# Score products of two attention branches: the low-part product over all 128 rows of the array instead of 64

## The chip, the cores and the metric

The kernel runs on one core of one Trainium2 chip. The metric is the time of one execution on the device, in microseconds. The engines of the core are called PE (TensorE, with PEld for its weight loads), DVE (VectorE), ACT (ScalarE), POOL (GpSimd) and SP (SyncE, which here only starts transfers).

## The reference

One step of a two-layer network on 128 context tokens and 512 latent tokens of width 1024. Every layer has a mixing sub-layer and a feed-forward sub-layer, each between two norms and modulated by a conditioning vector. The mixing sub-layer has three branches: A, grouped-query attention in a window (8 query heads, 2 key heads, a learned sink); B, attention over an 8 x 16 neighbourhood of a grid of 64 columns (8 heads, a learned bias); and C, a Fourier transform. All heads have 64 channels. The change is in the scores of branches A and B:

```python
s_band = jnp.einsum('bnqkgd,bnskd->bnkgqs', qb, kb, preferred_element_type=jnp.float32) * scale   # A
s_ctx = jnp.einsum('bnqkgd,bpkd->bnkgqp', qb, ck, preferred_element_type=jnp.float32) * scale
s_loc = jnp.einsum('bnqhd,bmnshd->bhnqms', q_blk, k_reg, preferred_element_type=jnp.float32) * scale  # B
s_ctx = jnp.einsum('bnqhd,bphd->bhnqp', q_blk, ck, preferred_element_type=jnp.float32) * scale
```

Each is followed by a softmax over the local and the context keys together, and by the product with the values.

## The kernel before

All dense products are computed with operands split in two parts: x = hi + lo, where hi has the reduced precision that one pass of the array takes and lo is the rest. A dense product is three passes: hi x hi (L487), hi x lo (L488) and lo x hi (L489), accumulated in one PSUM tile `ps_mm`. Weights arrive in pieces of 128 x 1024 on SP's queue; ACT makes their hi part (L144) and DVE their lo part (L145). Tokens are in two groups, of 384 and 256 columns, so most dense products stream 384 or 256 columns against 128 x 128 weights.

The scores are computed for a pair of heads at a time. `stack_q` (L591) builds `qst`, one 128-row operand for each head h of the pair: the 64 rows of the head's own half hold the hi part of q, the other 64 rows the lo part. A score is then two products into one tile `ps_s`. L547 takes all 128 rows of `qst` against all 128 rows of `khi`: this gives q_hi x k and q_lo x k. L548 takes only the 64 rows of q_hi against the 64 rows of `klo` and adds q_hi x k_lo. So L547 contracts over 128 rows of the array, and L548 over rows 0 to 63 (first head) or 64 to 127 (second head).

A unit of attention is one block of 128 queries for both heads of a pair: L547, L548, L547, L548, on 512, 384 or 128 key columns. There are 80 units: for each of the two layers, four pairs of branch A and four of branch B, with five units each. A unit goes through four steps, each emitted one tick after the other (`tick`, L516): the scores with a reduction on DVE (L549, maximum; POOL negates it in L551), the exponentials (ACT L557, DVE L562 and L564), the transposes of the probabilities (PE L574 into `ps_t`, copied by ACT L578 and DVE L576), and the product with the values (PE L587, which fills 64 columns of the array for each head). The ticks are interleaved with dense products: `step` (L228) counts the dense time that has been emitted, and lets a tick run when 2.5 us have gathered. All engines run their instructions in the order of this emission, which is written by hand.

For a pair of branch B, `queue_b` (L932) prepares the keys and the bias. ACT writes the hi part of the head's own half of `khi` (L940), DVE the lo part in `klo` (L941) and a copy of k in the other half of `khi` (L942). POOL clears a part of the bias tile (L945), starts eight transfers that fill the rest (L949), and adds the column mask (L956). `khi` and `klo` share one pool of two buffers (tag "k7"), so the next pair's `klo` takes the place of the last one's. In branch B `klo` is declared for two heads, and its first slot is used: rows 0 to 63 for the first head and rows 64 to 127 for the second. In branch A, `klo` has the lo part of a key head in both halves of the rows already (L734, L735).

Of the kernel before, what the change touches and what calls it, by code (L numbers as in the profile page):

```python
# [15 lines left out]
L = 2  # L16
# [29 lines left out]
class Null:  # L46
    """Stands for everything while the order of the weights is recorded."""
# [29 lines left out]
class Weights:  # L77
    """Streams pieces of [128, 1024] in the order of their use. A piece is one DMA and, but for raw ones,
    is split into two float32r parts (hi + lo) on chip."""
# [14 lines left out]
    @staticmethod  # L94
    def alt_slot(key):
        """Pieces that are split into a place of their own: of the token-major products the last one of the first half
        and the first one of the second, and what comes first after those products."""
        l, kind, n = key[:3]
        if kind in ("wo", "fo"):
            k0 = 0 if kind == "wo" else DFF // 128 - 8  # L100
            return {(0, k0 + 6): 0, (1, k0): 1}.get(key[2:])
        return 0 if n == 0 and (kind == "fg" or kind == "uc" and l) else None

    @staticmethod
    def is_side(key):
        """Pieces of w_ada that are used beside the feed-forward products have slots of their own."""
        return key[1] == "ada" and (key[0] > 0 or key[2] == 5)
# [68 lines left out]
    def early(self, key):  # L176
        """Moves a piece up in the order of the loads."""
        if self.recording:
            self.get(key)
# [17 lines left out]
class Kernel:  # L197
# [16 lines left out]
    # ---------------------------------------------------------------- order of emission  # L214
# [3 lines left out]
    def run_tasks(self, tags=()):  # L218
        """Those that are due; of some tags all; with tags None all."""
        while True:  # L220
            due = [t for t in self.tasks if tags is None or t[0] <= self.vt or t[2] in tags]
            if not due:
                return
            t = min(due, key=lambda z: z[0])
            self.tasks.remove(t)
            t[1]()

    def step(self, dur):  # L228
        """Called after dense products that take the tensor engine dur microseconds: emits what runs beside them."""
        self.vt += dur  # L230
        self.run_tasks()
        self.ada_acc += dur
        while self.ada is not None and self.ada_acc >= self.ada_dt:
            if next(self.ada, "end") == "end":
                self.ada = None
            self.ada_acc = self.ada_acc - self.ada_dt if self.ada_dt else -1.0
        if self.att_busy():
            self.acc += dur
            if self.acc >= TICK:
                self.acc = 0.0  # L240
                self.tick()

    # ---------------------------------------------------------------- pools
# [10 lines left out]
    # ---------------------------------------------------------------- weights  # L254
    def source(self, key):
        """DRAM pattern [128, a, b] of a piece and its b."""
# [22 lines left out]
    # ---------------------------------------------------------------- setup  # L279
# [34 lines left out]
    # ---------------------------------------------------------------- modulation  # L314
    def ada_round(self, l, r, acc=None):
        """1024 columns of silu(c) @ w_ada + b_ada for both token kinds: rounds 0 and 1 have half each of the first
        two blocks of D columns, the others a block each. Row 32j + s (s: 0 context, 1 latent) of a [128, 256] tile
        holds columns 256 j .. of kind s. With acc [128, 2, 1024] VectorE adds up the row blocks of w_ada, scaled, and
        TensorE only sums over the partitions."""
# [56 lines left out]
    def ada_columns(self, l, r, mod):  # L376
        """Columns of round r as [128, 8, 2]: channel 128 k + p of kind s, as is or (1 + it) * g."""
# [31 lines left out]
    # ---------------------------------------------------------------- norms  # L409
    def rstd(self, a, b=None):  # L410
        """(a + b) ** -0.5; b is EPS unless given."""
# [8 lines left out]
    def open_o(self):  # L420
        """A branch's result, split."""
# [3 lines left out]
    def norm_tiles(self):  # L425
        """Working space for the norms, in the same place."""
        return self.fix.tile([128, 5, D], F32, name="nt", tag="os", bufs=1)

    def pre_sq(self, t, x, z):
        """1 / rms(x[t])"""  # L430
# [4 lines left out]
    def pre_e(self, t, x, z, r):  # L435
        """z = x[t] / rms(x[t])"""
        self.nc.vector.tensor_scalar(z, x[:, t, :], r, None, op0=OP.mult)

    def pre_t1(self, l, sub, t, z, hfs, vec=False):
        """z transposed, by halves of the channels, and modulated."""  # L440
# [19 lines left out]
    def pre_t2(self, t, z, hfs, lo_on=None):  # L460
        """hT[:, t]: its two parts."""
# [8 lines left out]
    def square(self, t, h, src):  # L470
        """Mean square of half h of token tile t."""
# [7 lines left out]
    # ---------------------------------------------------------------- dense  # L479
    def mm_group(self, ps, lhs, rhs, g, K, ks=None):  # L480
        """ps = sum_k lhs_k.T @ rhs_k over the tokens of group g, in three float32r passes."""
# [14 lines left out]
    def proj(self, key, g, evac, parts=1):  # L496
        """128 columns of hT.T @ w for the tokens of group g; evac(psum, g) takes the result."""
# [17 lines left out]
    # ---------------------------------------------------------------- attention pipeline  # L515
# [16 lines left out]
    def drain(self, *key):  # L532
        """Until every unit whose key begins like this is through."""
# [3 lines left out]
    def att_s(self, u):  # L537
# [5 lines left out]
        for h in range(2):  # L543
            ps = self.psum("s")[:, :n]
            r0 = 64 * h
            out = ps if not u["grid"] else ps.rearrange("p (r c) -> p r c", c=32)
            nc.tensor.matmul(out, u["q"][:, h, u["qc"]], u["khi"](h), start=True, stop=False)  # L547
            nc.tensor.matmul(out, u["q"][r0:r0 + 64, h, u["qc"]], u["klo"](h), start=False, stop=True)  # L548
# [42 lines left out]
    def stack_q(self, stage):  # L591
        """Per head of a pair: rows of its own half hold hi, the other half lo."""
# [16 lines left out]
    def rope(self, dst, src, c0, n, scale):  # L609
        """dst = rotated src (PSUM), latent positions c0 .. c0 + n."""  # L610
# [10 lines left out]
    def rope_evac(self, dst, scale, c_lat):  # L621
        """Evacuates 128 rows of transposed q or k: context tokens as they are, latent ones rotated."""
# [8 lines left out]
    # ---------------------------------------------------------------- mixing sub-layer  # L631
# [7 lines left out]
    def mix_open(self, l):  # L639
        """First products on the tokens of group 0, beside the norms of the others."""  # L640
# [7 lines left out]
    def first(self):  # L648
        """The first norm and the first products of the first layer beside the modulation they need, in the order of
        START: A next piece of w_ada, F columns of a round, G / X loads, E moves a piece of uc up, P norm of a token  # L650
        tile, h / H first or second half of its channels modulated, l / L and split, S split of a piece of uc, m / M and
        n / N its products with either half for the tokens of group 0 and 1."""
# [169 lines left out]
    # ---- branch A  # L822
# [15 lines left out]
    def queue_a(self, p):  # L838
# [4 lines left out]
        # key columns (own context, cached, latent, cached), first mask tile and value tiles of each query block  # L843
# [3 lines left out]
        for b, ((k0, k1), m0, vt) in enumerate(spans):  # L847
# [5 lines left out]
                klo=lambda h, k0=k0, k1=k1: klo[64 * h:64 * h + 64, kv, k0:k1],  # L853
# [5 lines left out]
    # ---- branch B; latent columns of q are in blocks of 16 grid columns  # L859
# [72 lines left out]
    def queue_b(self, p):  # L932
# [5 lines left out]
        for h in range(2):  # L938
            a, b = slice(64 * h, 64 * h + 64), slice(64 - 64 * h, 128 - 64 * h)
            nc.scalar.activation(khi[a, h, :], ks[a, :896], AF.Copy)  # L940
            nc.vector.tensor_tensor(klo[a, 0, :], ks[a, :896], khi[a, h, :].bitcast(F32), op=OP.subtract)  # L941
# [18 lines left out]
        for n in range(4):  # L960
# [5 lines left out]
                klo=lambda h, s=s: lat(klo[64 * h:64 * h + 64], 0, s),  # L966
# [6 lines left out]
            khi=lambda h: khi[:, h, 0:128], klo=lambda h: klo[64 * h:64 * h + 64, 0, 0:128],  # L973
# [3 lines left out]
    # ---- branch C  # L977
    def load_dft(self, l):
        """The split position DFT, in the place of m until the branches are merged."""
# [20 lines left out]
    def four1(self, g):  # L1000
        """Channel DFT of group g, the cosine rows 0 .. 64 and the sine rows 1 .. 63 of it (the others are these or
        their negatives), then sums and differences of tokens 256 apart."""
# [31 lines left out]
    def mirror(dst, src):  # L1034
        """Pieces of all rows of a channel DFT, cosines and sines in the order 0 .. 64, 127 .. 65, from 65 + 63 of them."""
# [3 lines left out]
    def four2(self, g):  # L1039
        """Position DFT of group g: even frequencies from the sums, odd ones from the differences."""  # L1040
# [23 lines left out]
    # ---- gates and branch projections  # L1064
    def gates(self, br, ns):
        """tanh(half the gate) for output tiles ns, one group of tokens at a time."""
# [7 lines left out]
    def merge(self, br, n0, hook=None, gates=None):  # L1074
        """Output tiles n0, n0 + 1: m += 2 sigmoid(gate) * (o @ w_branch); the 2 goes when m is split."""
# [37 lines left out]
    # ---------------------------------------------------------------- token-major products  # L1113
# [27 lines left out]
    def xstat(self, keys, lhs, done):  # L1141
        """[128 tokens, 512] = sum of lhs_k[t].T @ w_k over the pieces of each half; done(t, half, psum)."""
# [15 lines left out]
    def xstat_tiles(self, keys, lhs, done):  # L1158
        """The same, with the second half token tile by token tile, so that the tiles end one after the other."""
# [44 lines left out]
    def tail(self, l, sub, t, z):  # L1204
        """x[t] += rms_norm(y) * g_post * gate, from z = y * g_post * gate, and, for sub-layer (l, sub), the next
        modulated norm."""
# [39 lines left out]
    # ---------------------------------------------------------------- feed-forward  # L1246
    def ffn(self, l):
        nc = self.nc
        n0 = 0
        for p, nt in enumerate(FFN_PARTS):  # L1250
# [3 lines left out]
            def split_of(j, aT=aT):  # L1254
                """hi and lo of row block j of the hidden layer."""
# [73 lines left out]
    # ---------------------------------------------------------------- all  # L1329
# [127 lines left out]
```

## Time and profile before

| | |
|---|---|
| median of 3 runs | 2252.7 us (2252.53 to 2252.97) |
| profiled execution, first to last instruction | 2250.8 us |
| the median less the profiled execution | 1.9 us |
| PE busy, PEld busy | 2213.2 us, 2008.8 us |
| DVE, ACT, POOL busy | 1137.3 us, 790.5 us, 337.9 us |
| attention units, first and last start | 124.6 us and 1628.0 us |

The time of the profiled execution is given as its span; what lies around the span in a timed run is the 1.9 us of the third row. A row of the timeline gives the start and the duration in microseconds, then the engine, the line of the kernel, the operation, the tile written and the tiles read, and the shape: for a matmul `64*128 64x384` means 64 rows and 128 columns of the array, and 64 rows by 384 columns of moving data. The matmuls of PE overlap each other, since they are pipelined, and their ends are modelled. What one of them costs the stream is therefore read from start to start.

### The profile page before, as it was taken

To read this page: it belongs to the slowest core of one execution; us is meant where nothing else is said; L and a number is where in the kernel's file an instruction comes from. 1 tells how busy PE (TensorE), PEld (TensorE's weight loads), DVE (VectorE), ACT (ScalarE), POOL (GpSimd) and SP (SyncE) were. 2 spreads that over 40 slices of the span, in tenths; PEclk is the share of its full clock that TensorE was granted. 3 is DMA by queue.
4 is the path that set the end of the run, shared out by engine and by line. 5 is a ranking of instruction groups with operands and counts; after the bars stand their busy time and mean duration, and the time that the engine had idled before them with its cause. 6 is when DMAs were issued, how large, how long until landed. Compare 5 with 4: busy or idle time off the path is not lost. (4 is left out here: it accounts for less than half of the span.)

```text
span 2250.8 us, 35153 instructions
## 1 busy us (share of the span) xinstructions
PE 2213.2 (98%) x14260; PEld 2008.8 (89%) x14260; DVE 1137.3 (51%) x2025; ACT 790.5 (35%) x1640; POOL 337.9 (15%) x619
## 2 busy tenths in 40 slices
PE   6999999999999999999989999999999999999998
PEld 4988899998879899899879888999998898998996
DVE  3554564553356566666466555645443662332343
ACT  3634443432243222112256344434333522221221
POOL 3100123231121000000041002222211400000002
PEclk9999999999999999999999999999999999999999
DMA  7311123233644444443332112233324142222221
GB/s 264 115 48 47 52 66 89 70 89 122 208 134 157 133 140 141 150 141 108 108 107 84 43 57 58 65 80 73 79 66 159 40 158 75 76 76 75 76 80 71
DMA packets 250049, 223.78 MB, mean 99 GB/s; under 512 B 10016, under 2 KB 209728, under 8 KB 249632
## 3 DMA queue, kind: packets, MB, share of 16 engines
q1 hardware_dynamic: 243408, 209.60, 30.1%
q0 software_dynamic: 6048, 11.68, 2.5%
q8 instruction: 113, 1.85, 0.3%
q14 instruction: 48, 0.39, 0.1%
q10 hardware_dynamic: 432, 0.25, 0.0%
HBM read 214.91 MB, written 6.59 MB: 98 GB/s over the span
## 5 line engine op out<-in xcount | busy, mean ns | idle before, releaser
L487 PE MATMUL ps_mm<-hT_hi,whi 128*128 128x256 f32 (+1 forms) x2832 | 890.9, 315 | 1.5 <-DVE sg L1098 1.0
L489 PE MATMUL ps_mm<-hT_hi,wlo 128*128 128x256 f32 (+1 forms) x2832 | 877.2, 310 | 0.8 <-DVE wlo L145 0.7
L488 PE MATMUL ps_mm<-hT_lo,whi 128*128 128x256 f32 (+1 forms) x2832 | 876.6, 310 | 0.0
L487 PEld LDWEIGHTS ps_mm<-hT_hi,whi 128*128 128x128 f32 x2832 | 533.0, 188 | 20.1 <-issue 15.1
L489 PEld LDWEIGHTS ps_mm<-hT_hi,wlo 128*128 128x128 f32 x2832 | 532.8, 188 | 1.6 <-DVE wlo L145 1.6
L488 PEld LDWEIGHTS ps_mm<-hT_lo,whi 128*128 128x128 f32 x2832 | 533.1, 188 | 0.2
L145 DVE TENSOR_TENSOR wlo<-wraw,whi 128x1024 fp32r<-128x1024 f32 x253 | 312.5, 1236 | 413.1 <-ACT whi L144 411.6
L144 ACT ACTIVATE whi<-wraw 128x1024 fp32r<-128x1024 f32 x253 | 266.9, 1056 | 285.6 <-PE ps_mm L1138 170.4
L1136 PE MATMUL ps_mm<-whi,aT 128*128 128x512 f32 x400 | 158.5, 396 | 0.0
L1138 PE MATMUL ps_mm<-whi,aT 128*128 128x512 f32 x400 | 157.9, 395 | 0.0
L1137 PE MATMUL ps_mm<-wlo,aT 128*128 128x512 f32 x400 | 157.8, 395 | 0.0
L1272 ACT ACTIVATE aT<-sg 128x384 fp32r<-128x384 f32 x88 | 41.5, 471 | 259.3 <-DVE sg L1270 259.3
L1071 ACT ACTIVATE sg<-ps_mm 128x384 f32<-128x384 f32 x96 | 41.7, 436 | 236.9 <-PE ps_mm L489 236.7
L350 DVE SCALAR_TENSOR_TENSOR ada_acc<-ada_raw,ada_st,ada_acc 128x1024 f32<-128x1024 f32 x98 | 123.6, 1280 | 0.0
L487 PE MATMUL ps_mm<-o,whi 128*128 128x256 f32 (+1 forms) x384 | 122.5, 319 | 0.0
L488 PE MATMUL ps_mm<-o,whi 128*128 128x256 f32 (+1 forms) x384 | 118.9, 310 | 0.0
L489 PE MATMUL ps_mm<-o,wlo 128*128 128x256 f32 (+1 forms) x384 | 118.8, 309 | 0.0
L1266 ACT ACTIVATE sg<-ps_mm 128x384 f32<-128x384 f32 (+1 forms) x88 | 38.5, 438 | 194.8 <-PE ps_mm L489 194.8
L477 POOL TENSOR_SCALAR ss<-ss 128x1 f32<-128x1 f32 x20 | 6.7, 336 | 603.6 <-ACT junk L475 602.8
L1267 DVE SCALAR_TENSOR_TENSOR sg<-sg,ps_mm 128x384 f32<-128x384 f32 (+1 forms) x88 | 42.9, 487 | 104.4 <-ACT sg L1266 104.4
L557 ACT ACTIVATE P<-P,sm 128x384 f32<-128x384 f32 (+2 forms) x160 | 92.8, 584 | 5.4 <-POOL sm L551 5.4
L1136 PEld LDWEIGHTS ps_mm<-whi,aT 128*128 128x128 f32 x400 | 75.2, 188 | 18.5 <-ACT aT L1272 0.8
(207 smaller groups left out, 2883.4 us busy)
## 6 DMA issues: line engine op xcount, KB each, us to landing
wraw<-in_w_in SPq DMA_DIRECT2D x92, 512.0 KB, 3.9
wraw<-in_w_ffn_in SPq DMA_DIRECT2D x88, 512.0 KB, 3.8
ada_raw<-in_w_ada SPq DMA_DIRECT2D x56, 512.0 KB, 4.4
wraw<-in_w_ffn_out SPq DMA_DIRECT2D x44, 512.0 KB, 3.5
wraw<-in_w_ada SPq DMA_DIRECT2D x40, 512.0 KB, 4.7
wraw<-in_w_branch SPq DMA_DIRECT2D x24, 512.0 KB, 3.5
wraw<-in_w_out SPq DMA_DIRECT2D x16, 512.0 KB, 4.0
bias<-in_b_rpbT POOLq DMA_DIRECT2D x64, 96.0 KB, 4.8
```

The source lines that it names most:

```text
L144: nc.scalar.activation(hi[:, :u.n], u.raw[:, :u.n], AF.Copy)
L145: nc.vector.tensor_tensor(lo[:, :u.n], u.raw[:, :u.n], hi[:, :u.n].bitcast(F32), op=OP.subtract)
L350: nc.vector.scalar_tensor_tensor(acc[:, s, :], u.raw, c, acc[:, s, :], op0=OP.mult, op1=OP.add)
L487: nc.tensor.matmul(ps, wh, xh[:, c0:c1], start=(k == 0), stop=False)
L488: nc.tensor.matmul(ps, wh, xl[:, c0:c1], start=False, stop=False)
L489: nc.tensor.matmul(ps, wl, xh[:, c0:c1], start=False, stop=(k == K - 1))
L557: nc.scalar.activation(P[:, h, :n], P[:, h, :n], AF.Exp, bias=sm[:, 2 + h:3 + h], accum_out=sm[:, 4 + h:5 + h])
L1071: lambda ps, g: self.nc.scalar.activation(sg[:, GROUPS[g][0]:GROUPS[g][1]], ps, AF.Tanh, scale=0.5))
L1136: nc.tensor.matmul(ps, xh[:, tc], u.hi[:, i, :], start=st and i == 0, stop=False)
L1137: nc.tensor.matmul(ps, xh[:, tc], u.lo[:, i, :], start=False, stop=False)
L1138: nc.tensor.matmul(ps, xl[:, tc], u.hi[:, i, :], start=False, stop=sp and i == 1)
L1267: nc.vector.scalar_tensor_tensor(t, t, 1.0, ps, op0=OP.add, op1=OP.mult)
```

## The change

In both branches L548 (L547 in the new numbering) takes all 128 rows of `qst` and all 128 rows of `klo`. In branch A this adds the product q_lo x k_lo, since `klo` has the lo part in both halves. In branch B `klo` uses both of its slots, one for each head: the head's own half gets the lo part as before, and the other half is set to zero by a new POOL instruction, 64 x 896, for each head. Comments and docstrings are taken out as well, which moves no instruction; from line 545 on, line numbers are smaller by one up to line 940, and the same as before from line 942 on.

```diff
     def att_s(self, u):
         ...
         for h in range(2):
             ps = self.psum("s")[:, :n]
-            r0 = 64 * h
             out = ps if not u["grid"] else ps.rearrange("p (r c) -> p r c", c=32)
             nc.tensor.matmul(out, u["q"][:, h, u["qc"]], u["khi"](h), start=True, stop=False)
-            nc.tensor.matmul(out, u["q"][r0:r0 + 64, h, u["qc"]], u["klo"](h), start=False, stop=True)
+            nc.tensor.matmul(out, u["q"][:, h, u["qc"]], u["klo"](h), start=False, stop=True)
...
     def queue_a(self, p):
         ...
-                klo=lambda h, k0=k0, k1=k1: klo[64 * h:64 * h + 64, kv, k0:k1],
+                klo=lambda h, k0=k0, k1=k1: klo[:, kv, k0:k1],
...
     def queue_b(self, p):
         ...
         for h in range(2):
             a, b = slice(64 * h, 64 * h + 64), slice(64 - 64 * h, 128 - 64 * h)
             nc.scalar.activation(khi[a, h, :], ks[a, :896], AF.Copy)
-            nc.vector.tensor_tensor(klo[a, 0, :], ks[a, :896], khi[a, h, :].bitcast(F32), op=OP.subtract)
+            nc.vector.tensor_tensor(klo[a, h, :], ks[a, :896], khi[a, h, :].bitcast(F32), op=OP.subtract)
+            nc.gpsimd.memset(klo[b, h, :].bitcast(F32), 0.0)
             nc.vector.tensor_copy(khi[b, h, :], ks[a, :896])
...
-                klo=lambda h, s=s: lat(klo[64 * h:64 * h + 64], 0, s),
+                klo=lambda h, s=s: lat(klo, h, s),
...
-            khi=lambda h: khi[:, h, 0:128], klo=lambda h: klo[64 * h:64 * h + 64, 0, 0:128],
+            khi=lambda h: khi[:, h, 0:128], klo=lambda h: klo[:, h, 0:128],
```

The order of POOL's instructions at the preparation of the first pair of branch B, before (the last transfers of the values, then the bias; in brackets the engines and queues that an instruction waits for):

```order
L913 DMA vbt<-in_c_cvb 128x128 [waits PE_49]
L913 DMA vbt<-in_c_cvb 128x128 x2
L945 MEMSET bias 128x6x128
L949 DMA bias<-in_b_rpbT 16x6x256
L949 DMA bias<-in_b_rpbT 16x6x256 [waits DMASW2_49]
```

The same place in the changed kernel:

```order
L912 DMA vbt<-in_c_cvb 128x128 [waits PE_49]
L912 DMA vbt<-in_c_cvb 128x128 x2
L941 MEMSET klo 64x896 [waits PE_49,Pool_49]
L941 MEMSET klo 64x896
L945 MEMSET bias 128x6x128 [waits Pool_49]
L949 DMA bias<-in_b_rpbT 16x6x256
L949 DMA bias<-in_b_rpbT 16x6x256 [waits DMASW2_49]
```

Two instructions per pair stand ahead of the bias, 16 in all, and the first of them waits for PE.

The order of PE's instructions at the first unit of that pair, before (the end of one dense product, the unit, the start of the next):

```order
L489 MATMUL ps_mm<-hT_hi,wlo 128x384
L547 MATMUL ps_s<-khi,qst 128x384 [waits DVE_49,Activation_49]
L548 MATMUL ps_s<-klo,qst 128x384
L547 MATMUL ps_s<-khi,qst 128x384 [waits DVE_49,Activation_49]
L548 MATMUL ps_s<-klo,qst 128x384
L487 MATMUL ps_mm<-hT_hi,whi 128x256 [waits DVE_49,PE_49]
```

In the changed kernel:

```order
L489 MATMUL ps_mm<-hT_hi,wlo 128x384
L546 MATMUL ps_s<-khi,qst 128x384 [waits DVE_49,Activation_49]
L547 MATMUL ps_s<-klo,qst 128x384 [waits Pool_49]
L546 MATMUL ps_s<-khi,qst 128x384 [waits DVE_49,Activation_49]
L547 MATMUL ps_s<-klo,qst 128x384 [waits Pool_49]
L487 MATMUL ps_mm<-hT_hi,whi 128x256 [waits DVE_49,PE_49]
```

The order is the same; in the first unit of each pair of branch B, the two low-part products also wait for POOL. (The order gives the output's shape, so that 64 or 128 rows of contraction read alike.)

## Prediction

> **What bounds the kernel now.** I read the page first: busy shares, slices, and the chain that ended last.
>
> ```profile
> span 2250.8 us, 35153 instructions
> PE 2213.2 (98%) x14260; PEld 2008.8 (89%) x14260; DVE 1137.3 (51%) x2025; ACT 790.5 (35%) x1640; POOL 337.9 (15%) x619
> ...
> PEclk9999999999999999999999999999999999999999
> ...
> PE 46%; DVE 1%; ACT 0%; POOL 0%; issue 0%; DVEq 0%; POOLq 0%; ACTq 0%
> ```
>
> PE has work in 98% of the span, at the full granted clock, and of the 47% of the span that the chain could be followed through, 46 are PE. So time comes off this kernel where PE's stream gets shorter, and a busy PE may still be one that streams badly: matmuls overlap, and start to start is what counts. Next I read the timeline of PE around one attention unit of 384 columns.
>
> ```profile
> 316.30 0.28 PE L488 MATMUL ps_mm<-hT_lo,whi 128*128 128x256 f32 x1
> 316.41 0.28 PE L489 MATMUL ps_mm<-hT_hi,wlo 128*128 128x256 f32 x1
> 316.53 0.34 PE L547 MATMUL ps_s<-khi,qst 128*128 128x384 f32 x1
> 316.80 0.44 PE L548 MATMUL ps_s<-klo,qst 64*128 64x384 f32 x1
> 317.17 0.45 PE L547 MATMUL ps_s<-khi,qst 128*128 128x384 f32 x1
> 317.55 0.44 PE L548 MATMUL ps_s<-klo,qst 64*128 64x384 f32 x1
> 317.92 0.44 PE L487 MATMUL ps_mm<-o,whi 128*128 128x384 f32 x1
> 318.20 0.34 PE L488 MATMUL ps_mm<-o,whi 128*128 128x384 f32 x1
> 318.38 0.34 PE L489 MATMUL ps_mm<-o,wlo 128*128 128x384 f32 x1
> ```
>
> A dense product of 256 columns starts the next after 0.12 us, one of 384 columns after 0.18 (318.20 to 318.38). In the unit, products of the same 384 columns take 0.27, 0.37, 0.38 and 0.37, and the dense product behind it 0.28. None of these rows names a wait for another engine. The weight loads say what is lost.
>
> ```profile
> 316.30 0.19 PEld L489 LDWEIGHTS ps_mm<-hT_hi,wlo 128*128 128x128 f32 x1
> 316.41 0.19 PEld L547 LDWEIGHTS ps_s<-khi,qst 128*128 128x128 f32 x1
> 316.80 0.18 PEld L548 LDWEIGHTS ps_s<-klo,qst 64*128 64x128 f32 x1 [0.20 <-issue]
> 317.17 0.19 PEld L547 LDWEIGHTS ps_s<-khi,qst 128*128 128x128 f32 x1 [0.19 <-issue]
> ```
>
> The load for the first L547 begins at 316.41, while the product before it still runs; the load for L548 begins only at 316.80, with L548 itself, after 0.20 us in which the load path did nothing. So it is again at the next, from 64 rows back to 128. Where the shape of the array stays, a load is hidden under the product before; where it changes, it is not. That the shape is the cause, and not the tiles or the PSUM bank, I take from another place, where L587 fills only 64 columns of the array.
>
> ```profile
> 345.55 0.34 PE L488 MATMUL ps_mm<-hT_lo,whi 128*128 128x384 f32 x1
> 345.73 0.34 PE L489 MATMUL ps_mm<-hT_hi,wlo 128*128 128x384 f32 x1
> 346.00 0.88 PE L587 MATMUL ps_o<-PT,vbt 128*64 128x128 f32 x12
> ...
> 347.00 0.36 PE L487 MATMUL ps_mm<-hT_hi,whi 128*128 128x256 f32 x1
> 347.20 0.28 PE L488 MATMUL ps_mm<-hT_lo,whi 128*128 128x256 f32 x1
> ```
>
> From L489 to L587 it takes 0.27 instead of 0.18: the same 0.09 that the first L547 loses ahead of L548 (0.27). And a dense product keeps its 0.12 to 0.18 when only the PSUM tile changes: L489 of `ps_mm` to L547 of `ps_s` took 0.12 (316.41 to 316.53), no loss.
>
> **The change part by part.** First, PE. The row that counts the units:
>
> ```profile
> L547 PE MATMUL ps_s<-khi,qst x160: 305/427/502, 124.6 to 1628.0; 128*128 128x384 f32 x96, 128*128 128x512 f32 x32, 128*128 128x128 f32 x32
> ```
>
> Two L547 make a unit: 48 units of 384 columns, 16 of 512, 16 of 128. With all 128 rows in L548 the unit has one shape throughout, and it is that of the dense products.
>
> Units of 384 columns: from the first L547 to the L488 behind, 318.20 - 316.53 = 1.67 us. At one shape these are five products of 0.176, 0.88. Gain 0.79 us; 48 x 0.79 = 37.9. By the four changes of shape in the unit it is 0.20 for each.
>
> For 512 and 128 columns, with the spacing of their sizes elsewhere:
>
> ```profile
> 136.13 0.48 PE L547 MATMUL ps_s<-khi,qst 128*128 128x512 f32 x1
> ...
> 138.06 0.28 PE L488 MATMUL ps_mm<-hT_lo,whi 128*128 128x256 f32 x1
> ...
> 149.59 0.30 PE L547 MATMUL ps_s<-khi,qst 128*128 128x128 f32 x1
> ...
> 150.87 0.33 PE L488 MATMUL ps_mm<-hT_lo,whi 128*128 128x384 f32 x1
> ...
> 2199.96 0.40 PE L1136 MATMUL ps_mm<-whi,aT 128*128 128x512 f32 x1
> 2200.19 0.40 PE L1137 MATMUL ps_mm<-wlo,aT 128*128 128x512 f32 x1
> ...
> 75.75 0.39 PE L1007 MATMUL ps_s<-cc,uT 128*128 128x128 f32 x2
> 75.97 0.39 PE L1010 MATMUL ps_t<-cc,uT 128*128 128x128 f32 x2
> ```
>
> Units of 512: 1.93 us now. At one shape: four products of 0.23, one of 0.12 for the L487 of 256 columns, and 0.08 that the first product behind transposes loses anyway (347.00 to 347.20 is 0.20, where 0.12 is usual): 1.12. Gain 0.81; x 16 = 13.0.
>
> Units of 128: 1.28 us now. No row shows a split product of 128 columns in a steady stream, so I bound it. The straight line through 256 and 384 columns (0.12, 0.18) gives 0.06. Above, L1007 with 128 columns of full precision takes 0.11 each (75.75 to 75.97 for two). I take 0.11, the row with the same load and column count: 4 x 0.11 + 0.176 + 0.08 = 0.70, gain 0.58, x 16 = 9.3. With 0.06 it is 0.78 each, 12.5.
>
> Sum on PE: 37.9 + 13.0 + 9.3 = 60.2 us; with the short price 63.4.
>
> A rule speaks against hiding the load. The Trainium skill (TensorE: Matmul & The Clock Gate, Part 3, The mechanism) says in its list of what overlaps that a weight load runs beside matmuls in flight only when its row group differs. By that rule an L548 over all rows could not hide its load either, and the sum would be near nothing. The trace disagrees in the four rows of loads above: full-array loads of 0.19 us start 0.11 apart there.
>
> Second, DVE and ACT. L941 writes as many elements to another slot; nothing is added to their queues.
>
> Third, POOL. Per pair of branch B two clears of 64 x 896 go ahead of the bias.
>
> ```profile
> 271.14 0.32 PE L548 MATMUL ps_s<-klo,qst 64*128 64x128 f32 x1
> ...
> 280.52 0.77 POOL L945 MEMSET bias<- 128x768 f32 x1
> ...
> 289.04 7.27 POOL L956 TENSOR_TENSOR bias<-bias,colmask 128x256 f32<-128x256 f32 x6 [3.68 <-DMA bias<-in_b_rpbT]
> ...
> 315.06 0.56 DVE L549 CUSTOM_DVE_ANT_0 P<-ps_s,bias 128x384 f32<-128x384 f32 x1
> ```
>
> A clear of 768 elements a row took 0.77, so 896 take about 0.9, and two 1.8 us; by the dearest neighbour, L956 with 256 elements in 1.2 us each, up to 4.2 each and 8.5 for both. All eight transfers and the mask behind them come later by that. The mask ends at 296.3 and its first reader, L549, runs at 315.06: 18.8 us of cover here. The clears wait for PE's last reading of the old `klo`, at 271.5, and POOL gets there at 280.5, so this wait is over before it begins; and the new wait of PE for POOL is over by some 282 to 289, long before the unit whose reduction runs at 315.06. I cost it at nothing. With no cover, eight pairs would pay 1.8 each, 14 us.
>
> Fourth, what a faster PE runs into. Over this stretch of a branch B pair:
>
> ```profile
> 312.00:345.00 33.00, 33.00 (x222) 28.59 (x221) 20.29 (x52) 13.75 (x34) 8.00 (x16) 1.00 0.22 62
> ...
> 316.03 0.08 DVE L549 DVE_READ_ACCUMULATOR2_ANT sm<- 128x1 f32 x1
> ```
>
> DVE is busy 20.3 of 33.0 us and ACT 13.8; with five units shorter by 0.79, DVE has 20.3 of 29.0, 70%. PE refills `ps_s` (two buffers) when DVE has reduced it: that ended at 316.11 for the second head, and L547 for it came at 317.17, 1.06 us later; for the first head 315.6 against 316.53, 0.9. One unit's gain of 0.79 just fits. I allow 1 us in all for places where it doesn't.
>
> So 2250.8 - 60.2 + 1.0 = 2191.6 for the span, and 1.9 more around it, as the runs have over the profile: **2193.5 us**.
>
> **The rivals.** (1) *DVE gives part of it back.* The first unit of each of the 16 pairs meets a DVE that is still at the splits of q or at weights; if the next unit's L547 waits for `ps_s` there, that unit's 0.79 is lost: 16 x 0.79 = 12.6, 2205 us. For it: only 0.9 us of room at 316.53. Against it: DVE's 61% here, and 0.9 is still more than 0.79. Chance 0.10.
>
> (2) *The load stays exposed.* If the losses belong to the accumulation into `ps_s` or to the loads of `qst`, and not to the shape, L548 over 128 rows starts its load as late as now, the spacing stays 0.37, and nothing is gained: 2252.7. (The rule cited above from the Trainium skill's page on TensorE would end here too.) For it: L548 lasts 0.44 and L547 0.45 in the same unit. Against it: L587, of another shape and other tiles, loses the same 0.09. Chance 0.04.
>
> (3) *POOL holds the bias, and the kernel gets slower.* The clear writes the tile that DVE's L941 writes too. If it were held until L941 has run, POOL would stand from 280.5 to 306.5:
>
> ```profile
> L941 DVE TENSOR_TENSOR klo<-stage,khi x16: 1083/1087/1092, 306.5 to 1599.7; 64x896 fp32r<-64x896 f32 x16
> ```
>
> The bias takes from 280.5 to 296.3, 15.8 us; with 1.8 for the clears it is ready at 324.1, 9 us after 315.06, and PE stands with both `ps_s` full. Eight pairs: 72 us, less 60: 2252.7 + 12 = 2265. It decides from 7.5 us of delay a pair on (60 / 8). Against it: the order shows the clear waiting for PE and POOL only. Chance 0.03.
>
> **How the numbers follow.** Forecast 0.83, rivals 0.10, 0.04, 0.03. The forecast's own range is 2185 (the short price of 128 columns, and 4 us for losses at transposes that I left in) to 2200. The range given takes in rival 1 and DVE losses somewhat past it: 2184 to 2210. Times within 0.2% of before, 4.5 us, count as no change, about what a measurement here can tell. Faster: forecast and rival 1, 0.93; same 0.04; slower 0.03.
>
> **What would show it.** Right: in a unit of 384 columns the five starts are 0.18 apart, and loads for the low-part product have no 0.2 us of idle path ahead; the units of 512 columns at 0.23, those of 128 between 0.06 and 0.11; the two stretches of attention (124 to 518 and 1243 to 1636 us) shorter by about 30 us each and nothing else moved; POOL's clears near 0.9 us each, done long before the unit. Wrong: spacings of 0.37 that stay; PE rows that wait for `ps_s` behind L549; a mask that ends after its first reader could run.

## The result

The changed kernel takes 2194.2 us (median; 2191.9 to 2196.1), the kernel before, on the same chip, 2252.6. The ratio is 0.974, with a 95% interval of 0.973 to 0.976: 58 us less. The forecast was 2193.5.

### The profile page after: what moved, and what is told of

The parts are those of the page before. It is cut to its first block, busy times and chain, and to the rows that moved or that the text cites. A ratio compares the mean times of both kernels' runs of the same rounds, so it can differ in the third digit from the quotient of the medians.

```text
span 2194.3 us, 35177 instructions
## 1 busy us (share of the span) xinstructions
PE 2156.5 (98%) x14260; PEld 2006.2 (91%) x14260; DVE 1131.7 (52%) x2025; ACT 790.7 (36%) x1640; POOL 354.4 (16%) x635
## 5 line engine op out<-in xcount | busy, mean ns | idle before, releaser
L487 PE MATMUL ps_mm<-hT_hi,whi 128*128 128x256 f32 (+1 forms) x2832 | 885.8, 313 | 1.5 <-DVE sg L1098 1.0
L489 PE MATMUL ps_mm<-hT_hi,wlo 128*128 128x256 f32 (+1 forms) x2832 | 877.6, 310 | 0.4 <-DVE wlo L145 0.4
L488 PE MATMUL ps_mm<-hT_lo,whi 128*128 128x256 f32 (+1 forms) x2832 | 877.0, 310 | 0.0
L487 PEld LDWEIGHTS ps_mm<-hT_hi,whi 128*128 128x128 f32 x2832 | 533.3, 188 | 10.7 <-issue 6.0
L489 PEld LDWEIGHTS ps_mm<-hT_hi,wlo 128*128 128x128 f32 x2832 | 533.2, 188 | 0.9 <-DVE wlo L145 0.9
L488 PEld LDWEIGHTS ps_mm<-hT_lo,whi 128*128 128x128 f32 x2832 | 533.3, 188 | 0.6
L487 PE MATMUL ps_mm<-o,whi 128*128 128x256 f32 (+1 forms) x384 | 120.1, 313 | 0.0
L488 PE MATMUL ps_mm<-o,whi 128*128 128x256 f32 (+1 forms) x384 | 118.9, 310 | 0.0
L489 PE MATMUL ps_mm<-o,wlo 128*128 128x256 f32 (+1 forms) x384 | 118.8, 309 | 0.0
L1099 POOL TENSOR_TENSOR m<-m,sg 128x384 f32<-128x384 f32 x64 | 63.6, 1004 | 196.8 <-DVE sg L1098 196.7
```

The lines of the kernel that those rows point to most:

```text
L487: nc.tensor.matmul(ps, wh, xh[:, c0:c1], start=(k == 0), stop=False)
L488: nc.tensor.matmul(ps, wh, xl[:, c0:c1], start=False, stop=False)
L489: nc.tensor.matmul(ps, wl, xh[:, c0:c1], start=False, stop=(k == K - 1))
L1099: nc.gpsimd.tensor_tensor(m, m, s, op=OP.add)
```

## The profile after

The head of the page of the changed kernel, which answers to the rows shown first for the kernel before:

```profile
span 2194.3 us, 35177 instructions
PE 2156.5 (98%) x14260; PEld 2006.2 (91%) x14260; DVE 1131.7 (52%) x2025; ACT 790.7 (36%) x1640; POOL 354.4 (16%) x635
...
PE 46%; DVE 1%; ACT 0%; POOL 0%; issue 0%; DVEq 0%; POOLq 0%; ACTq 0%
```

PE has as many matmuls as before and 57 us less to do; it still bounds the kernel. The other engines have the instructions that they had, and POOL has 16 clears more (13.7 us).

Where the time went is read best from the two stretches with attention. In a table by stretches the first columns are the stretch and its length, then PE's busy time and count. Before, from the first unit of a layer to some point behind the last one:

```profile
124.00:518.00 394.00, 394.00 (x2704) 352.04 (x2703) 208.62 (x504) 160.46 (x393) 80.68 (x176) 1.00 0.25 65
1243.00:1636.00 393.00, 393.00 (x2697) 351.03 (x2696) 206.94 (x504) 160.44 (x393) 81.86 (x176) 1.00 0.25 65
```

The same work after (the same 504 instructions on DVE and 393 on ACT):

```profile
127.00:491.00 364.00, 364.00 (x2699) 348.73 (x2698) 205.24 (x504) 160.53 (x393) 89.56 (x184) 1.00 0.26 70
1215.00:1580.00 365.00, 365.00 (x2706) 349.70 (x2706) 204.70 (x504) 160.54 (x393) 89.17 (x184) 1.00 0.27 70
```

394 us became 364, and 393 became 365. When the start of each of PE's 14260 matmuls is set beside its start before, each layer's stretch is 29.3 us shorter, 58.6 in all. From 530 to 1210 us the difference grows by 0.5 us more, and behind 1640 it stays the same within 0.1. (For 3 us at 1157 it is up to 1.3 smaller, where the granted clock after was low; a wait that PE had there before takes this up again.) Ahead of the first attention 2.5 us are lost: 0.6 by 30 us, 0.7 more by 36 us, and 1.3 from 36 to 44 us. That is no work of the change, which touches nothing there. For the last part the granted clock was low for longer. In the same table the granted clock is the third number from the right. From 36 to 44 us it was 0.79 of full speed in the profiled execution before:

```profile
36.00:44.00 8.00, 7.08 (x48) 4.85 (x49) 4.41 (x12) 3.87 (x8) 1.28 (x1) 0.79 0.69 232
```

and 0.57 after, with 32 matmuls where there were 48:

```profile
36.00:44.00 8.00, 7.11 (x32) 5.24 (x36) 3.95 (x7) 3.71 (x7) 1.90 (x3) 0.57 0.62 203
```

Now the unit of 384 columns that opens the first pair of branch B, on PE's timeline after:

```profile
299.81 0.34 PE L546 MATMUL ps_s<-khi,qst 128*128 128x384 f32 x1
299.99 0.34 PE L547 MATMUL ps_s<-klo,qst 128*128 128x384 f32 x1
300.17 0.34 PE L546 MATMUL ps_s<-khi,qst 128*128 128x384 f32 x1
300.35 0.34 PE L547 MATMUL ps_s<-klo,qst 128*128 128x384 f32 x1
300.53 0.28 PE L487 MATMUL ps_mm<-hT_hi,whi 128*128 128x256 f32 x1
300.65 0.28 PE L488 MATMUL ps_mm<-hT_lo,whi 128*128 128x256 f32 x1
```

Each score product starts the next after 0.18 us, like a dense product. For the loads, all 160 of each kind in one row (last column: how long the load path did nothing ahead of them); first before, then after:

```profile
L547 PEld LDWEIGHTS ps_s<-khi,qst 128*128 128x128 f32 x160 | 30.0, 188 | 14.4 <-issue 9.5 <-DVE PT L576 1.9 <-DVE m L1096 0.9
L548 PEld LDWEIGHTS ps_s<-klo,qst 64*128 64x128 f32 x160 | 29.2, 183 | 28.8 <-issue 26.6
```

```profile
L547 PEld LDWEIGHTS ps_s<-klo,qst 128*128 128x128 f32 x160 | 30.4, 190 | 0.7
L546 PEld LDWEIGHTS ps_s<-khi,qst 128*128 128x128 f32 x160 | 30.2, 189 | 1.8 <-DVE sm L548 0.7 <-issue 0.3
```

The loads last as long as before (0.19 us), but 43 us of idle load path have become 2.5.

A unit of 128 columns on PE's timeline after:

```profile
149.01 0.31 PE L546 MATMUL ps_s<-khi,qst 128*128 128x128 f32 x1
149.15 0.28 PE L547 MATMUL ps_s<-klo,qst 128*128 128x128 f32 x1
149.26 0.28 PE L546 MATMUL ps_s<-khi,qst 128*128 128x128 f32 x1
149.37 0.28 PE L547 MATMUL ps_s<-klo,qst 128*128 128x128 f32 x1
```

A product of 128 columns takes 0.11. And on the timeline of the weight loads after, the place where DVE now holds PE up a little:

```profile
303.79 0.19 PEld L546 LDWEIGHTS ps_s<-khi,qst 128*128 128x128 f32 x1 [0.18 <-DVE sm L548]
```

In the second unit of this pair of branch B the load for the second head waits 0.18 us for DVE to have read `ps_s`. That happens in four pairs, 0.7 us in all (the row of L546 above).

POOL's timeline at the first pair of branch B, after, and the first reader of the bias on DVE's:

```profile
268.21 1.73 POOL L941 MEMSET klo<- 64x896 f32 x2
269.89 0.74 POOL L945 MEMSET bias<- 128x768 f32 x1
270.58 4.17 POOL L949 DMA_DIRECT2D bias<-in_b_rpbT  x8
278.45 7.00 POOL L956 TENSOR_TENSOR bias<-bias,colmask 128x256 f32<-128x256 f32 x6 [3.71 <-DMA bias<-in_b_rpbT]
```

```profile
302.69 0.56 DVE L548 CUSTOM_DVE_ANT_0 P<-ps_s,bias 128x384 f32<-128x384 f32 x1
```

The two clears take 1.7 us, and the mask ends 17.2 us ahead of the first reader of the bias. Over the eight pairs this room is 11.1 to 17.2 us. The mask is six instructions, and the first reduction needs only the first of them (shown with 28 clears below); counted to that one, the room is 14.6 to 23.5 us.

## The experiments

The theory: what was lost is 0.2 us at every change of the array's shape, whichever instruction makes it. The first rival: it is lost by something of the scores themselves (the 64-row product, the accumulation into `ps_s`, the loads of `qst`). The second: POOL's clears cost something, and the gain would be larger without them.

### Branch A alone

```diff
-            nc.tensor.matmul(out, u["q"][:, h, u["qc"]], u["klo"](h), start=False, stop=True)
+            r = slice(0, 128) if u["key"][0] == "A" else slice(64 * h, 64 * h + 64)
+            nc.tensor.matmul(out, u["q"][r, h, u["qc"]], u["klo"](h), start=False, stop=True)
...  (and the keys of branch B as in the kernel before)
```

> Only branch A's low-part products go to 128 rows; branch B keeps its 64 rows, one slot of klo and no clears on POOL. Shape theory (each change of the array's shape costs 0.20 us, four in a unit): 16 units of 384, 16 of 512 and 8 of 128 columns gain 0.79, 0.81 and 0.58 us, 30.2 us in all: 2222 us, with the stretch 124 to 275 us about 15 shorter and that of branch B, 312 to 518, as long as before. If the gain of the change came from branch B's keys (klo in two slots, zeros): no gain here, 2252.

Measured: 2222.2 us, ratio to before 0.986 (0.985 to 0.988). Set against the kernel before, matmul by matmul, PE gains 14.9 us between 106 and 282 us and nothing from 282 to 560 us, where branch B of layer 0 runs. Half of the units bring half of the gain, with no clear at all, and at the size worked out for branch A (30.2 us; 31.4 by the median of the kernel before in the same runs).

### The same 64-row products, next to each other

The kernel before, with its four products in another order:

```diff
+        pss = [self.psum("s")[:, :n] for h in range(2)]
+        outs = ...
         for h in range(2):
-            ps = self.psum("s")[:, :n]
+            nc.tensor.matmul(outs[h], u["q"][:, h, u["qc"]], u["khi"](h), start=True, stop=False)
+        for h in range(2):
             r0 = 64 * h
-            out = ...
-            nc.tensor.matmul(out, u["q"][:, h, u["qc"]], u["khi"](h), start=True, stop=False)
-            nc.tensor.matmul(out, u["q"][r0:r0 + 64, h, u["qc"]], u["klo"](h), start=False, stop=True)
-            nc.vector.tensor_tensor_reduce(...
+            nc.tensor.matmul(outs[h], u["q"][r0:r0 + 64, h, u["qc"]], u["klo"](h), start=False, stop=True)
+        for h in range(2):
+            nc.vector.tensor_tensor_reduce(...
```

> The kernel before, with its 64-row products, but in the order khi of head 0, khi of head 1, klo of head 0, klo of head 1: two changes of shape in a unit instead of four, the same products. Shape theory: 2 x 0.197 x 80 = 31.5 us less, 2221 us. Rival, each 64-row product costs its 0.2 us wherever it stands (rows, accumulation into ps_s or the load of qst): no gain, 2252. Shape theory with the two 64-row products running side by side, since they are on different rows and different banks: a further 48 x 0.176 + 16 x 0.231 + 16 x 0.11 = 13.9 us less, 2207; then the two low-part products start within 0.02 us of each other.

Measured: 2210.6 us, ratio 0.981 (0.979 to 0.983). The unit after, on its timeline (x2: two products in one row):

```profile
305.69 0.63 PE L546 MATMUL ps_s<-khi,qst 128*128 128x384 f32 x2
306.25 0.45 PE L549 MATMUL ps_s<-klo,qst 64*128 64x384 f32 x2
306.63 0.45 PE L487 MATMUL ps_mm<-o,whi 128*128 128x384 f32 x1
306.92 0.34 PE L488 MATMUL ps_mm<-o,whi 128*128 128x384 f32 x1
```

Both low-part products together take 0.38 us from start to start of what follows; in the records they start 3 or 4 ns apart in all 80 units. So two products on the two halves of the rows, into the two buffers of `ps_s`, run side by side at the price of one, and each pair has two changes of shape instead of four. Both gains together were put at 45.4 us; by the median of the kernel before in the same runs (2253.6), 43.0 came. The rival that each 64-row product carries its own 0.2 us is out: the products are the same ones. (The Trainium skill, TensorE: Matmul & The Clock Gate, Why this matters for your kernels, gives a start 4 ns or less apart for products on distinct row groups; this trace, with 3 or 4 ns, agrees.) This order is still 16 us slower than the changed kernel: its two changes of shape cost 0.39 us a unit, and running side by side saves 0.18.

### A change of shape where there is no attention

```diff
+            r = slice(0, 64 if halves and k == 4 else 128)
-            nc.tensor.matmul(ps, wh, xl[:, c0:c1], start=False, stop=False)
+            nc.tensor.matmul(ps, wh[r], xl[r, c0:c1], start=False, stop=False)
...  (`halves` is set for the gate products of the feed-forward)
```

> The changed kernel, and in each product of the feed-forward gate (22 column blocks, 2 token groups, 2 layers: 88 places) one L488 out of eight takes only 64 of its 128 rows; the other 64 rows' contribution of that low part is left out. No attention, no qst and no ps_s there, and no product more or fewer. Shape theory: two changes of shape at 0.197 us in each place, 88 x 0.394 = 34.7 us more than the changed kernel's 2194.2: 2229. Rival, the loss belongs to the scores (accumulation into ps_s, or the loads of qst): 2194, no difference. Rival, a product over 64 rows is dearer by itself and the product behind it is not: 88 x 0.2 = 17 us, 2212, and then only its own spacing is longer, not those before and behind it.

Measured: 2226.8 us, 32.6 more than the changed kernel, 0.37 a place, where 34.7 and 0.39 were expected; set beside the changed kernel matmul by matmul, the 88 places cost 33.7. One place on its timeline:

```profile
694.33 0.34 PE L490 MATMUL ps_mm<-hT_hi,wlo 128*128 128x384 f32 x1
694.50 0.34 PE L487 MATMUL ps_mm<-hT_hi,whi 128*128 128x384 f32 x1
694.77 0.44 PE L489 MATMUL ps_mm<-hT_lo,whi 64*128 64x384 f32 x1
695.14 0.44 PE L490 MATMUL ps_mm<-hT_hi,wlo 128*128 128x384 f32 x1
695.42 0.34 PE L487 MATMUL ps_mm<-hT_hi,whi 128*128 128x384 f32 x1
```

From start to start: 0.17, 0.27, 0.37, 0.28, as in the scores of the kernel before. It is the change of shape that costs, in a dense product too: about 0.09 on the product ahead of it and 0.10 on the one behind. The third theory, that only the 64-row product is dear, fails at 0.27 and 0.28. That the 0.2 us is the exposed weight load (0.18 us, with 0.2 of idle load path ahead of it) fits every row here, but no run takes the load apart from the rest of the change.

### More clears on POOL

```diff
-            nc.gpsimd.memset(klo[b, h, :].bitcast(F32), 0.0)
+            for _ in range(5):
+                nc.gpsimd.memset(klo[b, h, :].bitcast(F32), 0.0)
```

That makes ten clears for a pair; the second of the two runs has 14 in place of 5, which makes 28.

> The changed kernel, with POOL's clear of klo done five times for each head, ten for a pair instead of two: 8 x 0.855 = 6.8 us more of POOL ahead of the bias in each of eight pairs. Cover theory: the mask ended 11.1 to 17.2 us ahead of its first reader in the changed kernel, so nothing shows, 2194 us. If POOL's time ahead of the bias lies on the path: up to 8 x 6.8 = 55 us more, 2249.

> The changed kernel with 28 clears of klo for a pair instead of two: 26 x 0.855 = 22.2 us more of POOL ahead of the bias. In the changed kernel the mask ended 17.2, 11.1, 15.0, 11.4, 17.1, 11.3, 14.8 and 11.2 us ahead of its first reader. Cover theory: the excess is 5.0, 11.1, 7.2, 10.8, 5.1, 10.9, 7.4 and 11.0, 68.5 us in all, less what PE can still do before it needs ps_s or what DVE holds back, some 1 to 4 us a pair: 2230 to 2255. If something else hides the bias, no loss: 2196, as with ten clears.

Measured with ten clears: 2196.4 us (two runs), against 2194.2; the ratios to before are 0.975 and 0.974. So 54 us more of POOL's time moved the end by about 2. That is not quite nothing, for PE has a wait that the changed kernel has not (us in total, times, longest):

```profile
PE ps_s L546 <- DVE sm L548: 2.3, 2, 1.2
```

It stands at the second unit of the third pair of branch B in each layer, and the bias is no cause of it: the mask ends 5.6 us or more ahead of its first reader there. DVE is late. POOL's mask now runs at the same time as DVE's split of the keys, and the split takes longer (ns, shortest, median and longest of 16; first in the changed kernel, then with ten clears):

```profile
L940 DVE TENSOR_TENSOR klo<-stage,khi x16: 1084/1087/1092, 294.1 to 1546.8; 64x896 fp32r<-64x896 f32 x16
L940 DVE TENSOR_TENSOR klo<-stage,khi x16: 1084/1490/1583, 290.9 to 1547.8; 64x896 fp32r<-64x896 f32 x16
```

The copy behind it takes 1.07 us instead of 0.62. In the two third pairs this makes DVE 1.3 and 1.4 us late, and set matmul by matmul beside the changed kernel PE loses the same 1.3 and 1.4 us. The two profiled spans, 2194.5 and 2194.3 us, do not show it, because the one with ten clears was 3.2 us ahead by 124 us, before any clear.

With 28 clears: 2261.4 us, 67 more than the changed kernel, and slower than the kernel before (ratio 1.004, 1.002 to 1.005). PE's waits with 28 clears (us in total, times, longest):

```profile
PE ps_s L546 <- DVE sm L548: 50.2, 16, 7.2
```

The second pair of branch B on POOL's timeline:

```profile
327.38 26.04 POOL L942 MEMSET klo<- 64x896 f32 x28
...
363.04 4.14 POOL L957 TENSOR_TENSOR bias<-bias,colmask 128x256 f32<-128x256 f32 x6 [4.85 <-DMA bias<-in_b_rpbT]
```

On PE's, and in the table by stretches:

```profile
364.42 0.69 PE L546 MATMUL ps_s<-khi,qst 128*128 128x384 f32 x1 [6.28 <-DVE sm L548]
```

```profile
363.00:371.00 8.00, 5.54 (x25) 5.03 (x26) 1.71 (x7) 1.30 (x4) 5.98 (x9) 0.57 0.00 0
```

The chain is the one that the third rival described: the mask is late, DVE's first reduction waits for it, both buffers of `ps_s` stay full, and PE stands, 50.2 us in all. PE goes on at 364.42, before the mask ends at 367.18: in all eight pairs the first reduction starts 0.03 or 0.04 us behind the first of the mask's six instructions (here 363.80 after 363.76).

The remaining 17 us were not expected. In each of the six pairs where PE stops for 6 to 7 us, the granted clock goes to 0.5 while PE stands and stays there for 6.8 us once and 10.2 us five times (0.57 over the stretch shown, 1.00 ahead of it and behind), so that PE works at half speed on what follows. Set beside the changed kernel matmul by matmul, from 124 us on, 54 us come at the 16 products that wait (start to start, where the 50.2 counts idle time alone), 13 us at the products behind them at the halved clock, and 1 us elsewhere. So the room ahead of the bias is real, and its end lies between 7 and 22 us of delay a pair.

### The values over all 128 columns

The same idea at the other change of shape in a unit of branch A: the values stand between columns of zeros, and both heads accumulate into one tile.

```diff
-                nc.tensor.matmul(po[64 * h:64 * h + 64, :], u["v"](i, h), PT[:, h, i * 128:i * 128 + 128],
-                                 start=(i == 0), stop=(i == nk - 1))
+                nc.tensor.matmul(po if full else po[64 * h:64 * h + 64, :], u["v"](i, h), PT[:, h, i * 128:i * 128 + 128],
+                                 start=(i == 0 and not (full and h)), stop=(i == nk - 1 and not (full and h == 0)))
...
-        self.va = va = ap.tile([128, 12, 128], F32, name="va", tag="v", bufs=2)
+        self.va = va = ap.tile([128, 1600], F32, name="va", tag="v", bufs=2)
+        nc.gpsimd.memset(va.rearrange("p (a b) -> p a b", b=64)[:, 0:25:2, :], 0.0)
...  (the values are written between the zeros; `full` is true for branch A)
```

> The changed kernel, and in branch A the products with the values fill all 128 columns of the array too: the value tiles stand between columns of zeros, and both heads accumulate into one tile, instead of 64 columns for each head. No product of branch A's units changes the shape any more. Shape theory: a unit loses 0.09 going into these products, 0.05 behind them, and their 0.135 each become 0.11, as for transposes: about 0.30 us a unit for 3 or 4 key tiles, 40 units, 12 us less than the changed kernel: 2182. Rival, two products on separate column halves run side by side today, and full width costs twice: 6 x 0.11 against 0.81 us shows no room for that, but with the reference to the changed kernel's 2194 it would be 2194 or more.

Measured: 2209.5 us, 15.3 more than the changed kernel, where 12 less were expected. The products with the values for a block of four key tiles (x16: 8 products in two records each), in the changed kernel and here:

```profile
146.93 0.28 PE L489 MATMUL ps_mm<-o,wlo 128*128 128x256 f32 x1
147.13 1.09 PE L586 MATMUL ps_o<-PT,va 128*64 128x128 f32 x16
148.16 1.09 PE L573 MATMUL ps_t<-ident,P 128*128 128x128 f32 x8
```

```profile
145.77 0.28 PE L489 MATMUL ps_mm<-o,wlo 128*128 128x256 f32 x1
145.89 1.95 PE L587 MATMUL ps_o<-PT,va 128*128 128x128 f32 x16
147.67 1.04 PE L573 MATMUL ps_t<-ident,P 128*128 128x128 f32 x8
```

The way in is shorter as expected, 0.12 instead of 0.20 from L489. But the products take 1.78 instead of 1.03. The expectation took 0.11 for a product, from the transposes; a product of full precision takes two records of 0.11, 0.22, and on 64 columns the eight products took 0.129 each: in the single records they start in pairs 6 or 7 ns apart, as the two heads' products do when they run side by side. So the same trade comes out the other way: here the narrow shape halves sixteen records for two changes of shape, and pays. The best of all these kernels remains the changed one.

## Why the prediction was right

*What bounds the kernel.* Right: what PE gained, the end gained. From the first score product of a unit to the second dense product behind it, the 80 units gained 58.5 us, against 60.2 less 1.0 in the forecast. The three terms came out at 36.7 (384 columns), 12.7 (512) and 9.1 (128), where 37.9, 13.0 and 9.3 were put.

*Units of 384 columns.* Forecast 0.79 each. The unit shown takes 0.84 from its first product to L488 behind it (299.81 to 300.65), where it took 1.62 before (312.19 to 313.81, four products of 384 columns and one of 256): 0.78. Over all 48 it is 0.76.

*Units of 128 columns.* The chosen price of 0.11 was measured as 0.11 (149.15 to 149.26); the short price of 0.06 was wrong, and with it a part of the range's low end. (That end was put at 2185, where 3.2 and 4 us off 2193.5 give 2186.) From 256 to 128 columns a product with its own load hardly gets cheaper here (0.12 and 0.11), and L1007 of the kernel before showed it.

*The cause.* The step that named the shape, and not the tiles or the bank, stood on one other place, L587. The dense products with 64 rows show it where nothing of the attention runs, and the adjacent order shows that the price goes by changes, not by products.

*POOL at nothing.* Right; two clears took 1.7 us (estimate 1.8), in front of 11 to 17 us of room. The price without cover was put at the bare delay, and this was too low where PE stops for long: with 28 clears the end moved 67 us where PE waited 50. What the working left out is that a longer POOL also meets DVE: with ten clears DVE's splits slowed down beside the mask and PE lost 2.7 us, though the bias was never late.

*Rival 1, DVE gives back.* Its place was right and its size was not. At the second unit of the pair shown the first head's room of 0.9 us shrank to 0.1. The second head's 1.06 us had to take 0.79 from the unit ahead and 0.28 from its own unit's first half, and its load waited 0.18 us. That came in four of the 16 pairs: 0.7 us was given back, not 12.6. The 1 us that the forecast allowed covers it.

*Rival 2, the load stays exposed.* Out, by the rows of loads after. *Rival 3* was not what the change did: the clears of the first pair were over at 269.9 us, and DVE first wrote `klo` at 294.1. With 28 clears the late bias stopped PE as that rival described, and the kernel was slower than before.

*What the sum did not contain* is the start, which differs from one execution to the next. By 124 us, where no run differs from the changed kernel, the profiled executions with ten clears and with dense 64-row products were 3.2 and 0.9 us ahead of it. The runs of the changed kernel spread over 4.2 us. So the mechanism and the terms were right, but that the forecast lies within 0.7 us of the median is in part luck.

## What to carry to other kernels

On PE, read start to start, not the duration: L548 and L547 lasted 0.44 and 0.45 in the same unit and both hid 0.2 us that was not theirs. In these kernels a product on part of the array was worth its two changes of shape (0.39 us together) only where enough of them stood next to each other on different parts and ran side by side: the 16 records of the values were, two score products were not. A lone one between full products was better filled up, with zeros or with the part that was there anyway. Before filling up, ask what the spare part was doing: the values' products were using it.

## What the runs showed of the hardware

With 28 clears PE stood for 6 to 7 us in six pairs, and in each the granted clock was halved for 6.8 or 10.2 us, from within the stop on (0.57 over 363 to 371 us; 1.00 before and behind). In the two pairs where it stood for 0.4 and 1.4 us, the clock stayed full. At the start of the program such a stretch lasted 3.4 us in the profiled execution before and 6.8 us in the one after, and the same products there ended 1.3 us later.

A change of shape costs the same 0.09 ahead and 0.10 behind for 64 rows by 128 columns as for 128 rows by 64 columns. For the second, the changed kernel has a place with a dense product on either side:

```profile
192.45 0.28 PE L489 MATMUL ps_mm<-hT_hi,wlo 128*128 128x256 f32 x1
192.66 0.44 PE L586 MATMUL ps_o<-PT,va 128*64 128x128 f32 x4
193.03 0.44 PE L487 MATMUL ps_mm<-hT_hi,whi 128*128 128x384 f32 x1
193.31 0.33 PE L488 MATMUL ps_mm<-hT_lo,whi 128*128 128x384 f32 x1
```

L489 of 256 columns takes 0.21 instead of 0.12, and L487 of 384 columns 0.28 instead of 0.18.

DVE's subtraction on 64 x 896 took 1.08 us alone and up to 1.58 while POOL's mask ran (ten clears), and its copy 0.62 and 1.07. While POOL's clears ran (28 clears), the subtraction kept its 1.08 to 1.09, and the copy took up to 1.39.
